# One order for all steps of a squared-ReLU MLP, and another tile order in its last block

## The chip, the cores and the metric

The kernel runs on one core of a Trainium2 chip. The metric is the time of one execution on the device in microseconds (us); a smaller one is better. The work of a core is done by TensorE (PE in the profile; its weight loads are the row PEld), VectorE (DVE), ScalarE (ACT), GpSimd (POOL) and SyncE (SP, which here only asks for transfers). Each of them runs its own instructions in order; they wait for one another by semaphores. Every matmul product lands in PSUM, which has eight banks of 512 float32 values a partition.

## What is computed

A trunk of two layers on 512 tokens of width 1024. Each layer has a mixer (latent attention in layer 0, gated linear attention in layer 1) and then this MLP:

```
def sq_relu_mlp(xn, w_up, w_down):          # 1024 -> 4096 -> 1024
    hid = jnp.square(jax.nn.relu(xn @ w_up))
    return hid @ w_down

x = x + sq_relu_mlp(rms_norm(x, norm_mlp[i]), mlp_w_up[i], mlp_w_down[i])
...
return rms_norm(x, final_norm)               # after layer 1
```

All of it is float32. The change touches the two MLPs and nothing else.

## The kernel before

**Numbers in two halves.** A float32 operand goes to TensorE as two pieces, a rounded high half and the rest as a low half. `split` makes them: ACT copies with rounding (L124), then VectorE subtracts (L127; L870 and L871 for a negated operand). A product of two such operands takes three matmuls (high x high, high x low, low x high). For weights the halves are the tiles `wh` and `wl`, four rooms of each (`piece`); for hidden values there are four rooms in `parts_room`, used in turn by `parts_of_quad`.

**Blocks and steps.** The 4096 hidden columns are cut into eight blocks of 512 (`FB`). `up_first` makes the first hidden block, `q11, q12, q21, q22` (two halves of its columns by two halves of the tokens). Then seven steps, b = 0 to 6, each do two things: the *down* products of the hidden block at hand, and the *up* products that make the next hidden block. Both use a scheme with 7 products in place of 8 (Strassen's, in Winograd's form), so a step has seven `up_product` and seven `down_product`, with sums of weights and of hidden values between them. The eighth block is done last, by itself.

**Up products.** They are called by the piece of tokens that they use: "11", "T1", "T2", "21", "T3", "22", "T4" (`quad`). Their weights are `A1` (with halves a11, a12), `A2` (s3, a22) and `S1` (s1); a11 becomes a11 + S1 before "T2", and a12 becomes a12 + a11 before "22". Their matmuls are at L993. Results are in banks of tag "u" (four of them), copied by ACT from one to another where two sums share a beginning (`y` is begun as a copy of `z`, `w2` as one of `w`), and end in `finish`: a rectifier on VectorE (L885) and a square on ACT (L886).

**Down products.** Weights `d11`, `d12`, `dS1`, `dS3`, `d22`; results go to the two-bank tiles "d" and "e" (or a pair of "u" banks), and from there to five running totals `S11, S12, S21, SU, S5`. Their matmuls are at L1006 in layer 0 (256 columns a matmul) and L1013 in layer 1 (512 columns).

**Two orders of a step.** `step`, used for b = 0 in each layer, alternates up and down products. `step_in_halves`, used for b = 1 to 6, does all up products first and then all down products. In both, `after(name)` follows the last use of a weight tile and asks for the next step's weights in the same place. `S1`, `A2`, `dS1` and `dS3` are each a sum of two parts of the weights: SP asks for the first, and POOL then asks for a transfer that adds the second.

**The start of an MLP.** `up_first` ends in four rectifiers (L900) and squares (L902). `quadrants` makes T1 to T4 on VectorE. `residual` loads the totals with the residual stream; in layer 1 by 32 transposes on TensorE (L941). Then the first step's weights are fetched in a list's order.

**The last block of layer 1.** The seventh step's last down products complete S12 (L1189) and then SU (L1192); S11 is complete before (L1179). `parts_of_quad` splits the four hidden quarters. For each of two column halves c and four tiles t of 128 tokens, `row(t, c)` adds 12 matmuls (L1303) to a bank that ACT has loaded with the total: for c = 0 S12 in "e" (tiles 2 and 3, L1272) and S11 in "d" (tiles 0 and 1, L1288), for c = 1 "u" banks (L1294). Then come the final norm's sums (L1306 to L1317) and the two stores of the tile (L1321, L1323).

The order in which each engine gets its instructions is set when the kernel is built: a planner takes them in the order of the program, and puts ahead those that are ready while others wait, by its own costs.

Of the kernel before, what the change touches and what calls it, by code (L numbers as in the profile page):

```python
# [14 lines left out]
AF = mybir.ActivationFunctionType  # L15
# [35 lines left out]
def trunk_kernel(ctx: ExitStack, tc: tile.TileContext, t_in: dict, out: bass.AP):  # L51
# [24 lines left out]
    def bank(tag):  # L76
        return psum["pool"].tile([P, 512], F32, tag=f"ps_{tag}", bufs=psum["banks"][tag], name=uname("ps"))

    def two_banks(tag):
        return psum["pool"].tile([P, 1024], F32, tag=f"ps_{tag}", bufs=1, name=uname("ps2"))  # L80
# [749 lines left out]
    def mlp(layer, nrm, nxt=None):  # L830
# [17 lines left out]
        def laid(t):  # L848
            return t.rearrange("p (j t) -> p j t", t=TH) if nxt else t
# [135 lines left out]
        def up_product(t, a, q, start):  # L985
            w = piece(a, KH, 256, at=AT_UP)
            for j in range(2):
                o = t[:, j * TH : (j + 1) * TH]
                for k in range(KH):
                    wh, wl = cut(w, slice(None), k, slice(j * P, (j + 1) * P))  # L990
                    xh, xl = quad[q][k][:, 0], quad[q][k][:, 1]
                    for n, (a_, x_) in enumerate(((wh, xh), (wh, xl), (wl, xh))):
                        PE.matmul(o, a_, x_, start=start and j == 0 and k == 0 and n == 0, stop=k == KH - 1 and n == 2, skip_group_check=True)  # L993
# [21 lines left out]

        def step(b, q, r, after):
            (q11, q12), (q21, q22) = q

            def begun(src):
                t = two_banks("e")  # L1020
                ACT.activation(t, src, AF.Copy)
                return t

            def add(total, t):
                DVE.tensor_tensor(total, laid(t), total, ALU.add)

            def onto(tag, total, a, parts, fresh=False):
                t = two_banks(tag)
                if not fresh:
                    ACT.activation(laid(t), total, AF.Copy)  # L1030
                down_product(t, a, parts, fresh)
                ACT.activation(total, laid(t), AF.Copy)

            A1, A2, s1 = W["A1"], W["A2"], W["S1"]
            a11, a12, s3, a22 = A1[:, :KH], A1[:, KH:], A2[:, :KH], A2[:, KH:]
            d11, d12, ds1, ds3, d22 = (W[n] for n in ("d11", "d12", "dS1", "dS3", "d22"))

            z = bank("u")
            up_product(z, a11, "11", True)
            y = bank("u")  # L1040
            ACT.activation(y, z, AF.Copy)

            d = two_banks("d")
            down_product(d, d11, parts_of_quad(q11), True)
            e = begun(d)

            up_product(y, a12, "21", False)
            finish(y, 0, 0, r)
            DVE.tensor_tensor(a11, s1, a11, ALU.add)

            down_product(e, d12, parts_of_quad(q21), False)
            add(S11, e)
            DVE.tensor_tensor(d11, ds1, d11, ALU.add)
            DVE.tensor_tensor(q12, q22, q12, ALU.subtract)
            DVE.tensor_tensor(q11, q11, q12, ALU.add)

            part = {"e": e}

            def down_11():
                down_product(d, d11, parts_of_quad(q11, -1.0), False)  # L1060
                part["e"] = begun(d)
                DVE.tensor_tensor(d12, d11, d12, ALU.add)
                after("d11")

            def up_t2():
                up_product(z, a11, "T2", False)
                u = part["u"] = tmp()
                ACT.activation(u, z, AF.Copy)
                DVE.tensor_tensor(a12, a11, a12, ALU.add)

            def up_t1():
                w = part["w"] = bank("u")
                up_product(w, s1, "T1", True)
                w2 = part["w2"] = bank("u")
                ACT.activation(w2, w, AF.Copy)  # L1075
                after("S1")

            def down_22():
                e = part["e"]
                down_product(e, d12, parts_of_quad(q22), False)  # L1080
                add(S12, e)
                after("d12")

            def down_12():
                down_product(d, ds3, parts_of_quad(q12), False)
                add(SU, d)
                after("dS3")
                DVE.tensor_tensor(q22, q22, q11, ALU.subtract)

            def up_22():  # L1090
                w = part["w"]
                up_product(w, a12, "22", False)
                c = tmp()
                DVE.tensor_tensor(c, w, part["u"], ALU.add)
                finish(c, 0, 1, r)
                after("A1")

            def up_t3():
                up_product(z, s3, "T3", False)
                v = tmp()  # L1100
                ACT.activation(v, z, AF.Copy)  # L1101
                c = tmp()
                DVE.tensor_tensor(c, part["w2"], v, ALU.add)
                finish(c, 1, 1, r)

            def down_5():
                onto("e", S5, ds1, parts_of_quad(q22, -1.0), True)
                after("dS1")
                DVE.tensor_tensor(q21, q21, q11, ALU.subtract)

            def down_21():
                onto("d", S21, d22, parts_of_quad(q21, -1.0))
                after("d22")

            def up_t4():
                up_product(z, a22, "T4", False)
                finish(z, 1, 0, r)
                after("A2")

            for product in (up_t2, down_11, up_t1, down_22, up_22, up_t3, down_12, up_t4, down_5, down_21):  # L1120
                product()

        def step_in_halves(b, q, r, after):
            (q11, q12), (q21, q22) = q
            A1, A2, s1 = W["A1"], W["A2"], W["S1"]
            a11, a12, s3, a22 = A1[:, :KH], A1[:, KH:], A2[:, :KH], A2[:, KH:]
            d11, d12, ds1, ds3, d22 = (W[n] for n in ("d11", "d12", "dS1", "dS3", "d22"))
# [2 lines left out]
                ACT.activation(dst, src, AF.Copy)  # L1130
                return dst

            def onto(total, a, parts):
                pair = [bank("u"), bank("u")]
                cols = [part_of(total, i) for i in range(2)]
                for p, c in zip(pair, cols):
                    copied(laid(p), c)
                down_product(pair, a, parts, False)
                for p, c in zip(pair, cols):
                    copied(c, laid(p))  # L1140

            w, w2, z, y = (bank("u") for _ in range(4))
            up_product(z, a11, "11", True)
            copied(y, z)
# [21 lines left out]
            after("A2")  # L1166

            d = two_banks("d")
            down_product(d, d11, parts_of_quad(q11), True)
            e = copied(two_banks("e"), d)  # L1170
            DVE.tensor_tensor(d11, ds1, d11, ALU.add)
            DVE.tensor_tensor(q12, q22, q12, ALU.subtract)
# [10 lines left out]
            after("d11")  # L1183
            p22 = parts_of_quad(q22)
            DVE.tensor_tensor(q22, q22, q11, ALU.subtract)
            onto(S5, ds1, parts_of_quad(q22, -1.0))
            after("dS1")
            down_product(e, d12, p22, False)
            DVE.tensor_tensor(S12, laid(e), S12, ALU.add)  # L1189
# [5 lines left out]
        up_first(Q[0])  # L1195
        quadrants()
        residual()
        for name in ("S1", "dS1", "d11", "A1", "d12", "dS3", "A2", "d22"):
            fetch(0, name)
        last_raw, last, gain = [], [[], []], []  # L1200

# [31 lines left out]
        for b in range(NB - 1):  # L1233
            final = b == NB - 2

            def after(name, b=b, final=final):
                if final:
                    return before_next(name) if nxt else at_the_end(name)
                fetch(b + 1, name)

            (step_in_halves if b else step)(b, Q[b % 2], Q[(b + 1) % 2], after)

        q = Q[(NB - 1) % 2]
        if nxt:
# [23 lines left out]
            es.close()  # L1268
            return
        hid = {}  # L1270
        loaded = {1: two_banks("e")}
        ACT.activation(loaded[1], S12, AF.Copy)  # L1272
        for h, th in ((0, 0), (0, 1), (1, 1), (1, 0)):
            hid[h, th] = parts_of_quad(q[h][th])
        DVE.tensor_tensor(S21, S21, SU, ALU.add)
        DVE.tensor_tensor(SU, SU, S5, ALU.add)
        rounded(1)
        gain = gain[0]
        DVE.tensor_scalar(gain, gain, -0.5, None, ALU.mult)
        stats = [sm(3) for _ in range(NT)]  # L1280
        rows = {}
        for c in range(2):
            for th in (1, 0):
                total = (S11, S12, S21, SU)[2 * c + th]
                if c == 0:
                    if th not in loaded:
                        loaded[th] = two_banks("d")
                        ACT.activation(loaded[th], total, AF.Copy)  # L1288
                    o = loaded[th]
                for i in range(2):  # L1290
                    cs = slice(i * 512, (i + 1) * 512)
                    if c:
                        o = bank("u")
                        ACT.activation(o, total[:, cs], AF.Copy, scale=-1.0)  # L1294
                    rows[2 * th + i, c] = total[:, cs], o if c else o[:, cs]

        def row(t, c):
            y, o = rows[t, c]
# [24 lines left out]
            ACT.dma_start(out_t[:, :512], y_0)  # L1323

        for c in range(2):
            for t in (2, 3, 0, 1):
                row(t, c)
        es.close()

# [554 lines left out]
```

## Time and profile before

| | |
|---|---|
| time, median of 3 runs | 1043.18 us (1042.81 to 1043.26) |
| time of the profiled execution | 1042.52 us |
| its span, first to last instruction | 1040.8 us |
| mean granted TensorE clock | 0.999 |
| busy: TensorE, weight loads, VectorE, ScalarE, GpSimd | 99%, 89%, 84%, 67%, 11% |
| MLP of layer 0: first step, the step after it | 39.39 us, 38.08 us |
| MLP of layer 1: first step with its transposes, the step after it | 42.68 us, 38.16 us |
| last block, first to last matmul's end | 1012.01 to 1034.3 us |

All times in the profile count from the first instruction. A line number is that of the kernel before, and can be that of a helper which many places call. "Idle before <- releaser" is the time for which the engine had nothing to do ahead of the instruction, and what it was waiting for last. A matmul's end is modelled, and a matmul starts while the one before it is still draining, so the distance from start to start tells what one costs.

### The profile page before, as it was taken

How to read it: one execution, taken by the hardware profiler on the slowest of the kernel's cores; microseconds unless marked ns; L12 is line 12 of the kernel's file. 1: busy time of each engine (PE TensorE's matmuls, PEld its weight loads, DVE VectorE, ACT ScalarE, POOL GpSimd, SP SyncE). 2: the span in 40 equal slices, each digit the busy share in tenths (PEclk: the TensorE clock that was granted, in tenths of full speed). 3: DMA queues.
4: the chain of work that ended last, by engine and by line, in shares of the span. 5: the costliest groups of instructions: out<-in, count | busy, mean ns of one | idle time of the engine just before them, and what ended most of it. 6: DMA issues, size and time to landing. Idle time of an engine off the chain costs nothing.

```text
span 1040.8 us, 16839 instructions
## 1 busy us (share of the span) xinstructions
PE 1030.6 (99%) x6522; PEld 923.2 (89%) x6522; DVE 878.5 (84%) x1343; ACT 695.1 (67%) x1122; POOL 113.2 (11%) x128
## 2 busy tenths in 40 slices
PE   9999999999999999999999999999999999999997
PEld 8788888899999999998888888888889989989985
DVE  7889976899989989989686499469898899898993
ACT  7667754667776876785345565655677677677684
POOL 8400000401101111000000000000011101111000
PEclk9999999999999999999999999999999999999999
DMA  7401214759988778623313212164488777878422
GB/s 234 123 21 41 78 45 148 200 134 223 234 195 204 180 198 203 150 82 122 91 41 95 95 54 82 51 163 148 98 239 203 188 199 191 203 182 198 106 82 82
DMA packets 120001, 145.85 MB, mean 140 GB/s; under 512 B 9488, under 2 KB 86288, under 8 KB 119920
## 3 DMA queue, kind: packets, MB, share of 16 engines
q1 hardware_dynamic: 95424, 113.57, 34.2%
q0 software_dynamic: 22400, 29.36, 17.8%
q10 hardware_dynamic: 2096, 1.84, 0.6%
q8 instruction: 51, 0.84, 0.3%
q14 instruction: 30, 0.25, 0.1%
HBM read 142.39 MB, written 2.10 MB: 139 GB/s over the span
## 4 chain that ended last, share of the span: by engine, by line
PE 92%; DVE 4%; ACT 2%; DMA 1%; issue 1%; SPq 0%; ACTq 0%; DVEq 0%
PE ps L993 25%; PE ps L1006 12%; PE ps L1013 12%; PE ps L132 10%; PE ps L133 10%; PE ps L134 10%; PE ps L1303 2%; PE ps L1264 2%; PE ps L149 1%; PE ps L1523 1%; PE ps L436 1%; PE ps L1650 1%; DVE wl L127 1%; ACT wh L124 1%; DMA comb<-in_mlp_w_down_dram 1%
## 5 line engine op out<-in xcount | busy, mean ns | idle before, releaser
L124 ACT ACTIVATE wh<-wraw 128x1024 fp32r<-128x1024 f32 x139 | 146.3, 1056 | 108.6 <-issue 37.0
L127 DVE TENSOR_TENSOR wl<-wraw,wh 128x1024 fp32r<-128x1024 f32 x139 | 169.5, 1220 | 36.6 <-ACT wh L124 35.8
L993 PE MATMUL ps<-T,wh 128*128 128x256 f32 x896 | 154.8, 275 | 0.1
L127 DVE TENSOR_TENSOR wl<-comb,wh 128x1024 fp32r<-128x1024 f32 x112 | 136.7, 1221 | 16.7 <-ACT wh L124 16.5
L124 ACT ACTIVATE wh<-comb 128x1024 fp32r<-128x1024 f32 x112 | 118.5, 1058 | 47.8 <-issue 28.8
L993 PEld LDWEIGHTS ps<-T,wh 128*128 128x128 f32 x896 | 135.1, 188 | 0.5 <-ACT tmp L1101 0.3
L993 PE MATMUL ps<-T,wl 128*128 128x256 f32 x448 | 123.3, 275 | 0.0
L1013 PE MATMUL ps<-wh,set 128*128 128x512 f32 x392 | 122.8, 390 | 0.2 <-ACT set L124 0.2
L993 PE MATMUL ps<-set,wh 128*128 128x256 f32 x672 | 117.0, 276 | 0.3 <-ACT ps L1075 0.2
L132 PE MATMUL ps<-set,wh 128*128 128x512 f32 x280 | 109.6, 391 | 0.0
L133 PE MATMUL ps<-set,wh 128*128 128x512 f32 x280 | 109.5, 391 | 0.0
L134 PE MATMUL ps<-set,wl 128*128 128x512 f32 x280 | 109.2, 390 | 0.0
L1006 PE MATMUL ps<-hidden_parts,wh 128*128 128x256 f32 x784 | 106.6, 275 | 0.0
L993 PEld LDWEIGHTS ps<-set,wh 128*128 128x128 f32 x672 | 101.9, 188 | 1.4 <-ACT ps L1075 0.4
L1006 PEld LDWEIGHTS ps<-hidden_parts,wh 128*128 128x128 f32 x784 | 97.0, 188 | 0.0
L993 PE MATMUL ps<-set,wl 128*128 128x256 f32 x336 | 92.6, 276 | 0.0
L1013 PEld LDWEIGHTS ps<-wh,set 128*128 128x128 f32 x392 | 73.5, 188 | 15.3 <-ACT set L124 0.4
L993 PEld LDWEIGHTS ps<-T,wl 128*128 128x128 f32 x448 | 84.1, 188 | 0.0
L1013 PE MATMUL ps<-wl,set 128*128 128x512 f32 x196 | 76.3, 389 | 0.0
L993 PEld LDWEIGHTS ps<-set,wl 128*128 128x128 f32 x336 | 63.1, 188 | 0.0
L134 PEld LDWEIGHTS ps<-set,wl 128*128 128x128 f32 x280 | 52.6, 188 | 11.0
L133 PEld LDWEIGHTS ps<-set,wh 128*128 128x128 f32 x280 | 52.6, 188 | 10.9 <-DVE set L765 0.2
(426 smaller groups left out, 2209.8 us busy)
## 6 DMA issues: line engine op xcount, KB each, us to landing
comb<-in_mlp_w_down_dram SPq DMA_DIRECT2D x74, 512.0 KB, 4.4
wraw<-in_mlp_w_up_dram SPq DMA_DIRECT2D x18, 1024.0 KB, 5.6
wraw<-in_mlp_w_up_dram SPq DMA_DIRECT2D x28, 512.0 KB, 5.8
comb<-in_mlp_w_down_dram POOLq DMA_DIRECT2D x28, 512.0 KB, 6.8
wraw<-in_gla_w_in_dram SPq DMA_DIRECT2D x12, 1024.0 KB, 5.2
comb<-in_mlp_w_up_dram SPq DMA_DIRECT2D x14, 512.0 KB, 4.6
comb<-in_mlp_w_up_dram POOLq DMA_DIRECT2D x14, 512.0 KB, 7.3
wraw<-in_mlp_w_up_dram POOLq DMA_DIRECT2D x14, 512.0 KB, 7.6
```

The lines of the kernel that those rows point to most:

```text
L124: order(ACT.activation(hi, src, AF.Copy))
L127: lo_eng.tensor_tensor(lo, src, f(hi), ALU.subtract)
L132: PE.matmul(psum, wh, xh, start=start, stop=False)
L133: PE.matmul(psum, wh, xl, start=False, stop=False)
L134: PE.matmul(psum, wl, xh, start=False, stop=stop)
L149: PE.transpose(psum, src, ident[: src.shape[0], : src.shape[0]])
L436: PE.matmul(p, w[:, i, j * P : (j + 1) * P], x, start=start, stop=stop)
L993: PE.matmul(o, a_, x_, start=start and j == 0 and k == 0 and n == 0, stop=k == KH - 1 and n == 2, skip_group_check=True)
L1006: PE.matmul(o, w_[:, k, j * P : (j + 1) * P], x_[:, ts], start=opens, stop=k == 1 and n == 2, skip_group_check=True)
L1013: PE.matmul(o, x_, w_, start=start and k == 0 and n == 0, stop=k == 1 and n == 2, skip_group_check=True)
L1264: PE.matmul(p, a, x, start=k == 0 and n == 0, stop=k == 3 and n == 2)
L1303: PE.matmul(o, a, b_, start=False, stop=k == 3 and n == 2, skip_group_check=True)
```

## The change

`step` is dropped, and `step_in_halves` takes its name and is used for every b. Three things are fitted to that:

- For b = 0 the split of `q11` stands ahead of the up products (`p11`); for b = 1 to 6 it stays at the first down product.
- `onto`, which loads a total into a pair of banks, adds a product and copies it back, can leave the loading out; for b = 0 it does so with S5, which is empty.
- The first step's weights are fetched in the order A1, S1, A2, d11, dS1, d22, d12, dS3.

In the last block of layer 1 the tiles go in the order 0, 1, 2, 3. The banks are loaded (`seed`) with S11 in two "u" banks for tiles 0 and 1, and S12 in the left half of "e" and the left half of "d" for tiles 2 and 3; for c = 1 in "u" banks as before, S21 first. The hidden quarters are split in the order (0, 0), (0, 1), (1, 0), (1, 1).

```diff
-        def step(b, q, r, after):
...
-            for product in (up_t2, down_11, up_t1, down_22, up_22, up_t3, down_12, up_t4, down_5, down_21):
-                product()
-
-        def step_in_halves(b, q, r, after):
+        def step(b, q, r, after):
...
-            def onto(total, a, parts):
+            def onto(total, a, parts, fresh=False):
                 pair = [bank("u"), bank("u")]
                 cols = [part_of(total, i) for i in range(2)]
-                for p, c in zip(pair, cols):
-                    copied(laid(p), c)
-                down_product(pair, a, parts, False)
+                if not fresh:
+                    for p, c in zip(pair, cols):
+                        copied(laid(p), c)
+                down_product(pair, a, parts, fresh)
...
+            p11 = None if b else parts_of_quad(q11)
             w, w2, z, y = (bank("u") for _ in range(4))
...
-            down_product(d, d11, parts_of_quad(q11), True)
+            down_product(d, d11, p11 or parts_of_quad(q11), True)
...
-            onto(S5, ds1, parts_of_quad(q22, -1.0))
+            onto(S5, ds1, parts_of_quad(q22, -1.0), b == 0)
...
-        for name in ("S1", "dS1", "d11", "A1", "d12", "dS3", "A2", "d22"):
+        for name in ("A1", "S1", "A2", "d11", "dS1", "d22", "d12", "dS3"):
             fetch(0, name)
...
-            (step_in_halves if b else step)(b, Q[b % 2], Q[(b + 1) % 2], after)
+            step(b, Q[b % 2], Q[(b + 1) % 2], after)
...
-        loaded = {1: two_banks("e")}
-        ACT.activation(loaded[1], S12, AF.Copy)
-        for h, th in ((0, 0), (0, 1), (1, 1), (1, 0)):
+        rows = {}
+
+        def seed(o, total, th, c, sign=1.0):
+            for i in range(2):
+                cs = slice(i * 512, (i + 1) * 512)
+                rows[2 * th + i, c] = total[:, cs], o[i]
+                ACT.activation(o[i], total[:, cs], AF.Copy, scale=sign)
+
+        seed([bank("u"), bank("u")], S11, 0, 0)
+        for h, th in ((0, 0), (0, 1), (1, 0), (1, 1)):
             hid[h, th] = parts_of_quad(q[h][th])
+        seed([split_banks("e")[0], split_banks("d")[0]], S12, 1, 0)
...
+        seed([bank("u"), bank("u")], S21, 0, 1, -1.0)
+        seed([bank("u"), bank("u")], SU, 1, 1, -1.0)
...
         for c in range(2):
-            for t in (2, 3, 0, 1):
+            for t in range(NT):
                 row(t, c)
```

More of the change, by code (lines that the diff above doesn't have):

```diff
@@ L1017, in step @@
             (q11, q12), (q21, q22) = q
[L1019 to L1043, printed above, removed]
-            down_product(d, d11, parts_of_quad(q11), True)
-            e = begun(d)
-            up_product(y, a12, "21", False)
@@ L1048, in step @@
[L1048 to L1118, printed above, removed]
-            for product in (up_t2, down_11, up_t1, down_22, up_22, up_t3, down_12, up_t4, down_5, down_21):
-                product()
@@ L1123, in step_in_halves @@
-        def step_in_halves(b, q, r, after):
-            (q11, q12), (q21, q22) = q
             A1, A2, s1 = W["A1"], W["A2"], W["S1"]
@@ L1168, in step_in_halves @@
             d = two_banks("d")
-            down_product(d, d11, parts_of_quad(q11), True)
+            down_product(d, d11, p11 or parts_of_quad(q11), True)
             e = copied(two_banks("e"), d)
@@ L1280, in mlp @@
         stats = [sm(3) for _ in range(NT)]
[L1281 to L1295, printed above, removed]
+        seed([bank("u"), bank("u")], S21, 0, 1, -1.0)
+        seed([bank("u"), bank("u")], SU, 1, 1, -1.0)
         def row(t, c):
```

## The prediction

> **What bounds the kernel now.** I read the page's busy row first, then the waits of TensorE, then the stages by windows, then the timeline at each place that the diff touches.
>
> ```profile
> PE 1030.6 (99%) x6522; PEld 923.2 (89%) x6522; DVE 878.5 (84%) x1343; ACT 695.1 (67%) x1122; POOL 113.2 (11%) x128
> ...
> L124 ACT ACTIVATE wh<-wraw 128x1024 fp32r<-128x1024 f32 x139 | 146.3, 1056 | 108.6 <-issue 37.0
> ```
>
> TensorE is busy for 99% of the span (the second row, the high half of a weight split on ACT, is for later). No matmul is added or dropped by the diff, so the only thing to win or lose is TensorE's idle time. Three of its waits (us in total, times, longest) lie inside the diff:
>
> ```profile
> PE ps L1303 <- ACT ps L1272: 1.0, 1, 1.0
> ...
> PE ps L993 <- ACT ps L1075: 0.2, 1, 0.2
> PE ps L1013 <- ACT set L124: 0.2, 1, 0.2
> ```
>
> The first is the last block, the second is the first step of layer 0, the third the first step of layer 1. "Busy" hides part of each loss (a matmul's modelled end overlaps the gap), so I size them by the length of whole stages:
>
> ```profile
> core 0: us, PE busy (x) PEld busy (x) DVE busy (x) ACT busy (x) POOL busy (x), PEclk, DMA share, GB/s
> 206.35:245.74 39.39, 38.99 (x337) 38.39 (x336) 38.80 (x44) 27.44 (x36) 5.34 (x5) 1.00 0.69 179
> 245.74:283.82 38.08, 38.08 (x338) 38.08 (x337) 35.27 (x40) 29.21 (x41) 5.00 (x4) 1.00 0.85 207
> ...
> 739.22:781.90 42.68, 42.50 (x286) 38.64 (x284) 35.77 (x41) 30.74 (x40) 4.97 (x4) 1.00 0.68 172
> 781.90:820.06 38.16, 38.16 (x254) 34.85 (x252) 33.97 (x37) 29.01 (x41) 3.80 (x3) 1.00 0.79 198
> ```
>
> Rows one and three are the first steps (b = 0, the interleaved `step`) of the two layers; rows two and four are the steps behind them (b = 1, `step_in_halves`), where TensorE is busy for all of the stage. The granted clock (PEclk) is 1.00 throughout. The diff gives b = 0 the order of b = 1.
>
> **Layer 0, first step.** It is the same 336 matmuls in 39.39 us instead of 38.08: 1.31 us lost. One of the three places in the timeline (start, us, engine, line; [idle before <- releaser]):
>
> ```profile
> 211.36 0.61 PE L1006 MATMUL ps<-hidden_parts,wh 128*128 128x256 f32 x4
> 212.04 0.50 PE L993 MATMUL ps<-set,wh 128*128 128x256 f32 x2
> ...
> 211.40 0.58 ACT L1041 ACTIVATE ps<-ps 128x512 f32<-128x512 f32 x1
> ```
>
> Four matmuls from 211.36 would be done streaming at 211.81 (a product of 24 takes 38.08/14 = 2.72 us, 0.113 us each); the next product starts at 212.04, behind the copy of `z` to `y` on ACT, which is used by the product but one after. In the new order three products lie between that copy and its use (T1, T2, then 21), so this wait goes. What must be ready instead: the low halves of S1 by the second product (206.35 + 2.72 = 209.07), of T2 by 211.79, of a12 by 214.51. The VectorE queue at that place:
>
> ```profile
> 204.27 1.21 DVE L127 TENSOR_TENSOR wl<-wraw,wh 128x1024 fp32r<-128x1024 f32 x1
> 206.13 0.69 DVE L127 TENSOR_TENSOR hidden_parts<-set,hidden_parts 128x512 fp32r<-128x512 f32 x1 [0.65 <-ACT hidden_parts L124]
> 206.74 1.22 DVE L127 TENSOR_TENSOR wl<-comb,wh 128x1024 fp32r<-128x1024 f32 x1
> 207.88 1.22 DVE L127 TENSOR_TENSOR wl<-wraw,wh 128x1024 fp32r<-128x1024 f32 x1
> 209.01 0.68 DVE L900 SCALAR_TENSOR_TENSOR tmp<-ps,rstd 128x512 f32<-128x512 f32 x1
> 209.62 1.21 DVE L1049 TENSOR_TENSOR wraw<-comb,wraw 128x1024 f32<-128x1024 f32 x1
> ```
>
> Start to start, a wide instruction costs 1.14 us and a narrow one 0.61. From 205.40 (behind a11's low half) the queue needs the sum a11 + S1 (1.14), q11's low half (0.61, the split moved ahead), L900 (0.61) and S1's low half (1.14): 208.9, against 209.07. That is just in time even in the worst order of the four, and the 0.65 us idle row shows VectorE had room there. T2's low half (1.14 more) comes at 210.0 to 211.2, against 211.79, with its ACT half (1.06) beside it. Over the whole up half VectorE needs 7 splits, 2 sums, 4 rectifiers and 2 adds, 9 x 1.14 + 6 x 0.61 = 13.9 of 19.04 us; the down half 12 x 1.14 + 11 x 0.61 = 20.4 of 19.04. The up half's surplus of 5.1 us, less 1.2 for L900 and q11's split, is the lead for the down half's shortage of 1.4. So I take 1.2 of the 1.31 us, keeping 0.1 for S1's narrow margin. Bounds: 1.31 gained; at worst two down splits (the rooms of `wh`, four, that a11 and S1 leave) and q11's split go ahead of an up split at a time without slack, 2 x 1.14 + 0.61 = 2.9 us lost, 1.6 worse than now.
>
> **Its transfers.** A1, S1 and A2 now stand first in SP's queue, and S1's and A2's accumulating parts first in POOL's. Two rows of POOL's timeline, two of the transfers (last number: us from issue to landing), one of ACT's timeline:
>
> ```profile
> 183.28 1.45 POOL L982 DMA_DIRECT2D comb<-in_mlp_w_up_dram  x1 [103.62 <-DMA comb<-in_mlp_w_up_dram]
> ...
> 191.82 1.80 POOL L971 DMA_DIRECT2D wraw<-in_mlp_w_up_dram  x1
> ...
> comb<-in_mlp_w_up_dram POOLq DMA_DIRECT2D x1, 512.0 KB, 6.2
> wraw<-in_mlp_w_up_dram POOLq DMA_DIRECT2D x1, 512.0 KB, 7.9
> ...
> 1006.59 0.59 ACT L1130 ACTIVATE sum<-ps 128x512 f32<-128x512 f32 x1
> ```
>
> S1 is whole at 183.28 + 6.2 = 189.5 and A2 at 199.7; A2 is wanted by the fifth product, at 217.2. The down operands move behind them, and are first wanted at 225. They cost nothing: A2 could come 17 us later. The totals' copies in halves are six instructions of 0.59 (the last row, such a copy in a later step) for three wide ones; even with nothing set against them ACT gets 3.5 us more, and it is busy for 27.44 of 39.39: nothing.
>
> **Layer 1, first step.** Of the 42.68 us the next step's 38.16 is work, and so are 32 transposes:
>
> ```profile
> 739.22 1.91 PE L941 MATMUL ps<-ident,xT 128*128 128x128 f32 x16
> 740.89 0.48 PE L993 MATMUL ps<-set,wh 128*128 128x256 f32 x2
> ...
> 753.60 0.28 PE L993 MATMUL ps<-T,wh 128*128 128x256 f32 x1
> 754.05 0.50 PE L1013 MATMUL ps<-wh,set 128*128 128x512 f32 x1 [0.18 <-ACT set L124]
> ...
> 768.18 0.39 PE L993 MATMUL ps<-T,wh 128*128 128x256 f32 x2
> ...
> 770.90 0.40 PE L1013 MATMUL ps<-wh,set 128*128 128x512 f32 x1
> ...
> 773.66 0.40 PE L993 MATMUL ps<-T,wh 128*128 128x256 f32 x2
> ```
>
> 16 transposes from 739.22 to 740.89 are 1.67 us, 32 are 3.34; 42.68 - 38.16 - 3.34 = 1.18 us lost. The wait for q11's split at 753.60 is 0.45 - 0.11 = 0.34, and the matmul behind it reads 0.50 where the row at 770.90 has 0.40: 0.10. A product behind one of its own kind takes 2.72 (768.18 to 770.90), behind one of the other kind 2.76 (770.90 to 773.66); the interleaved order changes kind 10 times, the new one twice: 8 x 0.04 = 0.32. I take these three, 0.76; the other 0.42 lies where transposes and products alternate, which the change leaves. Bounds: 1.18 gained, 2.1 lost (the same 2.9 of new stall, less 0.76).
>
> **Last block.** Rows of the timeline, and one of the chain (start, us, what):
>
> ```profile
> 1010.63 0.39 PE L1013 MATMUL ps<-wh,set 128*128 128x512 f32 x1
> 1012.01 22.31 PE L1303 MATMUL ps<-set,set 128*128 128x512 f32 x96 [0.99 <-ACT ps L1272]
> ...
> 801.14 19.07 PE ps L1013 x84
> ...
> 1000.64 1.22 DVE L1179 TENSOR_TENSOR xT<-ps,xT 128x1024 f32<-128x1024 f32 x1
> ...
> 1008.47 0.68 DVE L127 TENSOR_TENSOR set<-set,set 128x512 fp32r<-128x512 f32 x1
> ...
> 1009.67 1.22 DVE L1189 TENSOR_TENSOR xT<-ps,xT 128x1024 f32<-128x1024 f32 x1
> ...
> 1022.89 11.00 PEld L1303 LDWEIGHTS ps<-set,set 128*128 128x128 f32 x49 [0.32 <-DVE xT L1309]
> ```
>
> A matmul of this width takes 19.07/84 = 0.227 us, so TensorE stands from 1010.86 to 1012.01, 1.15 us: tiles 2 and 3 open on S12, whose last sum (L1189) and copy (L1272) come behind the last product but one. S11 is complete at 1001.86 (L1179) and the last "u" banks are free at 1007.2 (L1130's row above), so its two copies (0.59 each) end long before 1010.86; the third hidden split, now (1, 0), is the one that ends at 1009.2 (1008.47 + 0.68). The 96 matmuls take 22.31 instead of 95 x 0.227 + 0.39 = 21.96: 0.35, most of it around 1022.89, where a weight load waits for a read of the other half of its bank pair. I take 1.4 of 1.15 + 0.35. Bounds: 1.5 gained; nothing, if another late input takes over. New waits: S12's right half goes to d once L1192 has read it (about 1013.2); queued behind it on ACT is tile 0's Square, due at 1013.6. The fourth hidden split and S12 are wanted by tile 2 at 1016.3. Everything behind the last matmul stays, so this gain reaches the end whole.
>
> **The sum.** 1.2 + 0.76 + 1.4 = 3.36 us. The profiled execution took 1042.52 us (span 1040.8), so 1039.16; the median of the runs is 0.66 above it, 1043.18, which gives 1039.8.
>
> **The rivals.**
>
> 1. Layer 0 keeps its loss, since VectorE is the bound there: 38.80 of 39.39 us busy. Against it: four of its 44 instructions there belong to the next step, which has 40. Gain 0.76 + 1.4: 1041.0. Chance 0.12.
>
> 2. Taking the halves apart is the loss itself. Rows:
>
> ```profile
> 245.74:264.78 19.04, 19.04 (x170) 19.04 (x169) 16.93 (x20) 13.74 (x19) 1.30 (x1) 1.00 0.85 199
> 264.78:283.82 19.04, 19.04 (x170) 19.04 (x169) 18.34 (x22) 15.47 (x23) 3.70 (x3) 1.00 0.85 215
> ```
>
> VectorE is at 16.93 in an up half, at 18.34 in a down half; a first step that has no lead loses the 1.4 us of shortage in each layer: layer 0 stays within 0.1 of now, layer 1 gets 0.6 worse, the last block 1.4 better: 1042.5. The Trainium skill, Perfetto Trace Analysis, section Optimization Strategy, says that where the most contended engine changes over time, interleaving the regimes may help; this change does the opposite. By that rule this rival holds; the trace disagrees so far as b = 1 goes, whose down half has TensorE at 19.04 of 19.04. Chance 0.10.
>
> 3. The last block's wait only changes its name: the hidden split that ends at 1009.2 slips by 3 us (it is wanted at 1012.2, by the seventh matmul), or a seed does. Gain 1.2 + 0.76: 1041.2. Chance 0.09.
>
> 4. Slower: down splits placed ahead of up splits starve both first up halves, 2.9 us each: 5.8 - 3.36 = 2.4 over, 1045.6. It decides from 5.5 us of new stall in all. For it: VectorE has no idle row after 206.13 in layer 0. Against it: in layer 1 it has many, 35.77 of 42.68. Chance 0.05.
>
> **How the numbers follow.** The forecast (all three parts, 1038.8 to 1041.0) has 0.62, and 0.02 is left for what I don't see. A measurement of this kernel can tell 0.2%, 2.1 us, from no change: 1041.1 is the line. Faster is 0.62 and half of rival 1, 0.68; same the other half, rivals 2 and 3 and a rest, 0.26; slower 0.06. The range runs from all 1.31 + 1.18 + 1.5 gained with 0.4 us of scatter, 1038.8, to 1042.2, which takes in rivals 1 and 3.
>
> **What would show it.** The two first steps by windows: 38.1 to 38.3 us and 41.8 to 42.0 us; no wait on L993 or L1013 in them; the kind of product changing twice; the first matmul of the last block 0.23 us behind the last product, and 21.96 us for its 96. It is wrong if TensorE waits for a `wl` at the second or third product of layer 0, or for a hidden part or a seed at the last block.

## The result, and the profile after

| | before | after |
|---|---|---|
| time, median | 1043.28 us (20 runs, 1041.06 to 1045.27) | 1041.55 us (20 runs, 1040.58 to 1042.24) |
| profiled execution, its span | 1042.52, 1040.8 us | 1041.60, 1039.9 us |
| layer 0, first step | 39.39 us | 39.03 us |
| layer 1, first step with its transposes | 42.68 us | 43.71 us |
| layer 1 from its second step to the end | 258.9 us | 257.4 us |

The ratio is 0.9982, 95% interval 0.9975 to 0.9989: 1.9 us less, where 3.4 had been forecast. The time lies within the forecast's range, but 0.45 us above its line of 1041.1 us, on the side that it called "same" (chance 0.26). With 20 runs of each kernel the interval still leaves out "no change". Only one of the three terms came out as worked out. The two profiled executions differ by 0.9 us; where the rest of the gain of the medians is, the experiments below show in part.

From the page of after, the busy row:

```profile
PE 1028.7 (99%) x6522; PEld 922.0 (89%) x6522; DVE 878.8 (85%) x1343; ACT 695.8 (67%) x1130; POOL 113.6 (11%) x128
```

The matmuls are the same 6522. The stages of after by windows: the two first steps, and the down half of the last step of layer 1 (window and length, busy time and count of each engine, granted clock, DMA share, GB/s):

```profile
206.04:245.07 39.03, 38.47 (x338) 38.28 (x337) 38.27 (x43) 29.55 (x42) 4.99 (x4) 1.00 0.76 189
738.78:782.49 43.71, 42.30 (x286) 38.22 (x285) 36.06 (x41) 31.50 (x44) 3.44 (x4) 1.00 0.64 157
...
992.37:1011.45 19.08, 19.08 (x87) 15.77 (x86) 17.46 (x23) 17.07 (x28) 0.00 (x0) 1.00 0.34 110
```

The later steps run without a gap, as before. The second row is the one to stop at: layer 1's first step got 1.03 us longer. TensorE's waits in after (us in total, times, longest):

```profile
PE ps L1013 <- ACT ps L1023: 1.4, 1, 1.4
...
PE ps L993 <- ACT tmp L1023: 0.6, 1, 0.6
```

The waits named in the prediction (L1272, L1075, and the split of q11 for L1013) are all gone. Two new ones stand in their place, one in each first step, both for the copies of `copied` (L1023). The last block, in TensorE's timeline of after:

```profile
1011.22 0.39 PE L1013 MATMUL ps<-wh,set 128*128 128x512 f32 x1
1011.45 21.92 PE L1193 MATMUL ps<-set,set 128*128 128x512 f32 x96
```

It begins 0.23 us behind the last product, and its 96 matmuls take 21.92 us.

**The wait in layer 0.** Timeline of after, VectorE, then ACT, then TensorE:

```profile
217.46 0.68 DVE L871 SCALAR_TENSOR_TENSOR hidden_parts<-set,hidden_parts 128x512 fp32r<-128x512 f32 x1
218.07 1.22 DVE L127 TENSOR_TENSOR wl<-wraw,wh 128x1024 fp32r<-128x1024 f32 x1
219.20 0.68 DVE L871 SCALAR_TENSOR_TENSOR hidden_parts<-set,hidden_parts 128x512 fp32r<-128x512 f32 x1
219.81 0.68 DVE L885 SCALAR_TENSOR_TENSOR tmp<-ps,rstd 128x512 f32<-128x512 f32 x1
...
220.52 0.63 ACT L886 ACTIVATE set<-tmp 128x512 f32<-128x512 f32 x1 [1.35 <-DVE tmp L885]
221.06 0.58 ACT L1023 ACTIVATE ps<-xT 128x512 f32<-128x512 f32 x1
221.58 1.05 ACT L124 ACTIVATE wh<-comb 128x1024 fp32r<-128x1024 f32 x1
222.54 0.58 ACT L1023 ACTIVATE tmp<-ps 128x512 f32<-128x512 f32 x1
...
222.33 0.28 PE L993 MATMUL ps<-set,wl 128*128 128x256 f32 x1
223.16 0.50 PE L993 MATMUL ps<-T,wh 128*128 128x256 f32 x2 [0.56 <-ACT tmp L1023]
```

Read it backwards. The last up product, "T4", goes on in the bank of "T3" and must wait until ACT has copied that bank to `v` (222.54), 0.72 us beyond TensorE's own pace. ACT is late because its queue stood for 1.35 us at the square of product "21", and that waited for the rectifier of "21" on VectorE (219.81), 2.6 us after the product's last matmul had ended (217.2). Ahead of the rectifier VectorE was doing work for the *down* half: two of those instructions are shown (L871, halves of -q21 and -q11), six of 0.61 us in all stand between 210.5 and 219.8.

**The wait in layer 1.** The same three engines of after:

```profile
765.01 1.28 DVE L127 TENSOR_TENSOR set<-set,set 128x512 fp32r<-128x512 f32 x2
766.22 0.68 DVE L1070 TENSOR_TENSOR set<-set,set 128x512 f32<-128x512 f32 x1
...
763.75 1.21 ACT L124 ACTIVATE set<-set 128x512 fp32r<-128x512 f32 x2
764.86 1.01 ACT L1023 ACTIVATE ps<-ps 128x1024 f32<-128x1024 f32 x1
...
764.13 0.39 PE L1013 MATMUL ps<-wh,set 128*128 128x512 f32 x1
765.92 0.50 PE L1013 MATMUL ps<-wh,set 128*128 128x512 f32 x1 [1.41 <-ACT ps L1023]
```

The first down product ends at 764.36, and the second (d12, into "e") begins with a copy of the first's result; that copy can only start then, starts 0.5 us later (ACT is at two late splits) and lasts 1.01 us, and TensorE has nothing else. In later steps the product onto S21 stands between the two and covers the copy (in the next step the same copy runs from 804.84 to 805.85, and TensorE has no gap). Here its operand -q21 was not there: q21 is overwritten in place (L1070), so that sum must wait until the split of q21 has read it (765.01), and the split, though q21 was whole at 740.4, stands on ACT behind all squares of the up half (763.75). So -q21 is whole only at 769.2. Why the planner put this split last in layer 1 and not in layer 0 was not found out.

### The profile page after: what moved, and what is told of

It reads as the page before. It is cut to its first block, busy times and chain, and to the rows that moved or that the text cites. A ratio compares the mean times of both kernels' runs of the same rounds, so it can differ in the third digit from the quotient of the medians.

```text
span 1039.9 us, 16853 instructions
## 1 busy us (share of the span) xinstructions
PE 1028.7 (99%) x6522; PEld 922.0 (89%) x6522; DVE 878.8 (85%) x1343; ACT 695.8 (67%) x1130; POOL 113.6 (11%) x128
## 4 chain that ended last, share of the span: by engine, by line
PE 88%; DVE 5%; ACT 3%; DMA 2%; issue 1%; SPq 0%; ACTq 0%; DVEq 0%
PE ps L993 26%; PE ps L1013 13%; PE ps L1006 12%; PE ps L132 10%; PE ps L134 10%; PE ps L133 10%; PE ps L1413 1%; PE ps L149 1%; PE ps L1193 1%; DVE wl L127 1%; DMA wraw<-in_mla_w_in_dram 1%; PE ps L1540 1%; ACT wh L124 1%; DVE acc L266 1%; PE ps L1159 1%
## 5 line engine op out<-in xcount | busy, mean ns | idle before, releaser
L1013 PE MATMUL ps<-wh,set 128*128 128x512 f32 x392 | 122.3, 390 | 1.4 <-ACT ps L1023 1.4
L1013 PEld LDWEIGHTS ps<-wh,set 128*128 128x128 f32 x392 | 73.6, 188 | 17.2 <-ACT ps L1023 1.8
L1013 PE MATMUL ps<-wl,set 128*128 128x512 f32 x196 | 76.1, 389 | 0.0
L134 PEld LDWEIGHTS ps<-set,wl 128*128 128x128 f32 x280 | 52.6, 188 | 11.2 <-DVE wl L127 0.2
```

Source lines behind the costliest of these rows:

```text
L134: PE.matmul(psum, wl, xh, start=False, stop=stop)
L1013: PE.matmul(o, x_, w_, start=start and k == 0 and n == 0, stop=k == 1 and n == 2, skip_group_check=True)
```

## The experiments

**The two parts of the change, one at a time.** First the kernel before with the new last block:

> The kernel before, with only the last block's part of the change (its first two tiles first, their banks and copies). If the last block is what won, as the trace of after shows it (its 96 products stand directly behind the last product, where 1.15 us of wait and 0.35 us between the products were before), this alone is 1.4 to 1.5 us below before, and the two first steps stay at 39.4 and 42.7 us. Rival: what the last block wins depends on the new steps ahead of it; then it is under 1 us.

Measured: 1042.12 us against 1043.14 of before, ratio 0.9993 (0.9984 to 1.0001). The time alone does not settle it: a gain of 1.0 us by the medians and 0.7 by the ratio, with an interval from 1.7 down to nothing. The trace does: from the second step of layer 1 to the end it takes 257.4 us, as after does, so the block's gain does not need the new steps. Then the kernel after with the old last block:

> The kernel after, with the old last block: only the steps and their order of fetches are changed. By the two traces (first step of layer 0 0.36 us shorter, first step of layer 1 1.03 us longer) it is about 0.7 us slower than before, 0.3 to 1.0 with the scatter. By the prediction (1.2 and 0.76 us won) it would be 2.0 us faster. If it is within 0.2 us of before, the two profiled executions differ by something besides these two steps.

Measured: 1042.38 us against 1043.14, ratio 0.9992 (0.9983 to 1.0001); not slower. Its own first steps, by windows, are those of after:

```profile
208.05:246.90 38.85, 38.38 (x337) 38.18 (x336) 38.09 (x43) 29.53 (x42) 4.55 (x4) 1.00 0.77 190
740.66:784.32 43.66, 42.25 (x286) 38.19 (x284) 36.05 (x41) 31.50 (x44) 3.76 (x4) 1.00 0.64 157
```

That points at the other kernel: 39.39 us may not be the usual length of the old first step of layer 0. The run with the old steps and the new last block showed 40.03.

**The kernel before, profiled again.**

> The kernel before, unchanged, profiled once more. It asks how far its own stages move from one execution to the next: layer 0's first step took 39.39 us in the profile of before and 40.04 us in the kernel with only the new last block, which has the same step. If the old step moves by itself, this one shows another length, anything from 39.4 to 40.1 us, while the new step, which took 39.03, 38.86 and 39.04 us in three kernels, does not move. If it does not move, it is 39.4 us again, layer 1's first step 42.7 us, and the last block's wait 1.15 us.

> As the one before it: a third profile of the kernel before. Of interest are the length of the two first steps (39.4 to 40.0 and 42.7 us so far), the wait ahead of the last block (1.15 us in before, 0.39 us in the kernel with only the new steps, whose last block is the same), and the first 12 us, where one execution took 0.43 us from product to product for a while and another 0.23 us.

Layer 0's first step by windows, in the first of the two (the other took 40.11 us):

```profile
206.48:246.73 40.25, 38.98 (x337) 38.38 (x336) 39.03 (x45) 27.98 (x38) 5.54 (x5) 1.00 0.66 174
```

So the old step moves by 0.9 us from one execution to the next, and the profile on which the prediction rests holds the shortest of four. Layer 1's step does not move (42.71 and 42.70 us). What moves it is on ACT. The same row in the timeline of before, and in the first of the two others (in brackets, how long ACT was idle ahead of it, and what ended that):

```profile
201.73 1.07 ACT L124 ACTIVATE wh<-comb 128x1024 fp32r<-128x1024 f32 x1 [2.40 <-DMA comb<-in_mlp_w_down_dram]
```

```profile
202.70 1.07 ACT L124 ACTIVATE wh<-comb 128x1024 fp32r<-128x1024 f32 x1 [3.25 <-DMA comb<-in_mlp_w_down_dram]
```

This is the split of d11, the operand of the old step's second product. ACT, whose queue is in order, stands until the load has landed:

| execution with the old step | split of d11 starts | step ends | difference | step |
|---|---|---|---|---|
| before | 201.73 | 245.74 | 44.01 | 39.39 |
| new last block only | 202.06 | 246.07 | 44.01 | 40.03 |
| before, third | 202.45 | 246.42 | 43.97 | 40.11 |
| before, again | 202.70 | 246.73 | 44.03 | 40.25 |

The end of the step follows the landing to within 0.06 us. (The next expectation counts from 0.06 us ahead of the split's start, so its distances are that much longer.) To move the landing on purpose, d11 and d12 exchange their rooms in the old step, so that d11's load is issued second:

```diff
-        home = {"S1": 0, "dS1": 1, "d11": 4, "d12": 3, "dS3": 2, "d22": 5}
+        home = {"S1": 0, "dS1": 1, "d11": 3, "d12": 4, "dS3": 2, "d22": 5}
```

> The old steps (and the new last block), with the rooms of the weights d11 and d12 exchanged, so that d11 is loaded as the second of the four late transfers instead of the first, about 1.7 us later. Theory: the old first step of layer 0 is set by the landing of d11, the operand of its second product, since in four executions its end came 44.07, 44.09, 44.03 and 44.07 us behind the end of ScalarE's wait for d11, while the step took 39.39 to 40.25 us. Then the wait ends about 1.7 us later (203.7 to 204.4 us), the step takes 41 to 42 us and its end is again 44.0 to 44.2 us behind it. Rival: the landing is not what sets it; then the step stays at 39.4 to 40.3 us.

The step by windows, and ACT's row:

```profile
205.32:246.59 41.27, 39.24 (x338) 38.45 (x337) 38.98 (x44) 29.97 (x42) 6.19 (x5) 1.00 0.65 170
```

```profile
203.57 1.07 ACT L124 ACTIVATE wh<-comb 128x1024 fp32r<-128x1024 f32 x1 [5.34 <-DMA comb<-in_mlp_w_down_dram]
```

The split starts at 203.57, 1.75 us ahead of the step's start, where it was 3.78 to 4.62 ahead in the four: 2.0 to 2.9 us later. The step is 1.0 to 1.9 us longer than in the four, which is the same less 1.0; so the length came out as expected, the distance did not: from the split to the step's end it is 43.02, not 44.0. The missing 1.0 us fits a weight split of 1.04 us that stood close behind d11's on ACT (203.31 in before) and that the planner now put behind the squares and q11's split (206.90). So the landing sets the old step, through what stands behind it on ACT. The new step wants d11 only at its second half.

The old last block varies in the same way: TensorE's wait ahead of it was 1.15 us in before and 1.24, 0.41 and 0.39 us in three others; ACT's split of a last-block weight began 4.31 and 4.39 us behind the issue of its load in the first two, 3.56 and 3.54 in the others. That it follows the landing is read from these four alone; it was not tried.

**Layer 1: the hidden values ahead.** The kernel after, and for b = 0 of layer 1, ahead of the up products:

```diff
             p11 = None if b else parts_of_quad(q11)
+            if b == 0 and not nxt:
+                DVE.tensor_tensor(q12, q22, q12, ALU.subtract)
+                DVE.tensor_tensor(q11, q11, q12, ALU.add)
+                p21 = parts_of_quad(q21)
+                DVE.tensor_tensor(q21, q21, q11, ALU.subtract)
+                m21 = parts_of_quad(q21, -1.0)
```

> The kernel after, with four sums and splits of the hidden values moved ahead of the up products in layer 1's first step alone, so that the product onto S21 has its operand in time. Theory: the 1.57 us of wait behind the first down product is the copy of d to e, which nothing covers, as the product that covers it in later steps waits for its late operand. Then the wait goes, the first step of layer 1 falls from 43.7 to 42.0 us, and the whole is 1.5 to 1.7 us below after (3.4 to 3.6 below before). Rival: VectorE and ScalarE are simply full in a step whose halves are not interleaved; then the work moved ahead only moves the wait into the up products, the step stays at 43 to 44 us and the time within 0.4 us of after.

Measured: 1039.44 us against 1043.14, ratio 0.9970 (0.9958 to 0.9981). Windows, then VectorE's rows of the in-place sum and of -q21's low half, in this kernel:

```profile
738.75:780.74 41.99, 41.94 (x286) 38.38 (x284) 36.83 (x41) 31.05 (x44) 2.82 (x3) 1.00 0.67 162
```

```profile
743.89 0.69 DVE L1043 TENSOR_TENSOR set<-set,set 128x512 f32<-128x512 f32 x1
...
745.91 0.68 DVE L871 SCALAR_TENSOR_TENSOR set<-set,set 128x512 fp32r<-128x512 f32 x1
```

-q21 is whole at 746.6 instead of 769.2, no wait is left, and the step is 41.99 us, 1.72 less. VectorE does no less in it than in after (36.83 against 36.06 us), so its load was not the bound. Then only one of the moved pairs, the split of q21:

```diff
+            p21 = parts_of_quad(q21) if b == 0 and not nxt else None
...
-            p21 = parts_of_quad(q21)
+            p21 = p21 or parts_of_quad(q21)
```

> The kernel after, with one of the five moved instruction pairs only: the split of q21 ahead of the up products in layer 1's first step, the sums and the split of -q21 as they were. Theory: the product that must stand between the first down product and its copy needs the split of -q21, which comes last in the chain of sums, so one split alone does not help: the step stays above 43.0 us, with a wait of 1 us or more behind the first down product. Rival, that the late split of q21 itself (763.75 us) is the cause: the wait goes and the step falls to 42.0 to 42.3 us.

```profile
738.74:781.40 42.66, 42.47 (x286) 38.22 (x284) 36.72 (x41) 31.13 (x43) 2.99 (x3) 1.00 0.65 158
```

```profile
744.00 0.69 DVE L1071 TENSOR_TENSOR set<-set,set 128x512 f32<-128x512 f32 x1
...
765.07 0.68 DVE L871 SCALAR_TENSOR_TENSOR set<-set,set 128x512 fp32r<-128x512 f32 x1
```

I expected that it would not help; it brought 1.05 of the 1.72 us. The in-place sum followed by itself (744.00 instead of 766.22): once the split has read q21, the planner can put the overwriting sum where there is room. What stayed late is -q21's own split (765.07): TensorE, now at the product onto S21, stops shortly for its high half (until 764.47) and again for its low half (until 765.81), and this is the remaining 0.67. The step thus lies between the theory (above 43.0) and the rival (42.0 to 42.3): the larger part is the late read of a value that is overwritten in place, the smaller one the last split in the chain.

**Layer 0: the split ahead.** The kernel after without q11's split ahead, in both layers (`p11 = None`):

> The kernel after without the first down operand split ahead of the up products; everything else stays. Theory: the split ahead is not what delays layer 0's last up product (five other narrow instructions still stand ahead of the rectifier of product 21), so layer 0's first step stays within 0.4 us of 39.0 us, with the wait at the same product. In layer 1 the first down product loses its ready operand, so the step is as long or longer: 43.7 to 44.5 us. Rival, that the split is what crowds VectorE: both steps get shorter by about a split's two instructions, 0.7 us or more.

```profile
205.79:244.01 38.22, 38.22 (x337) 38.19 (x336) 38.05 (x44) 29.68 (x42) 4.99 (x4) 1.00 0.79 192
737.47:786.37 48.90, 44.24 (x286) 39.27 (x285) 37.95 (x42) 32.03 (x45) 3.22 (x4) 0.97 0.56 138
763.42:767.70 4.28, 3.67 (x10) 2.60 (x9) 3.44 (x6) 0.13 (x1) 0.00 (x0) 0.60 0.57 153
```

The theory missed in both layers. In layer 0 the step falls to 38.22 us: without that split at the head of VectorE's queue, the rectifier of "21" comes 12.97 us behind the step's start instead of 13.77, and that is enough. In layer 1 it costs 5.2 us, far more than the 0.8 expected at most; the third row, a part of this, is told of further down. The split ahead is thus worth 5.2 us in layer 1 and costs 0.8 in layer 0. The same in the other direction, with the sums and splits of q21 and -q21 ahead in layer 0 as well:

> The kernel with layer 1's sums and splits ahead, and the same edit in layer 0 as well. Theory: in layer 0 VectorE has no idle time while the up products run, so narrow instructions put ahead delay the rectifier of product 21 or a low half as before: layer 0's first step is 39.0 us or longer, up to 40 us, where it is 38.1 us with that work held back; layer 1 stays at 42.0 us. Rival: what matters in both layers is that the operands of the second down product are early; then layer 0's step falls to 38.2 us as well.

```profile
206.29:245.28 38.99, 38.66 (x337) 38.26 (x336) 38.23 (x43) 29.55 (x42) 4.76 (x4) 1.00 0.78 190
738.98:780.98 42.00, 41.94 (x285) 38.38 (x284) 36.83 (x41) 31.07 (x44) 3.01 (x3) 1.00 0.65 157
```

What gains 1.7 us in layer 1 gains nothing in layer 0: TensorE now waits for two earlier copies on ACT, ahead of 212.06 and 217.96.

**Both layers mended, in two ways.** Layer 1 with the hidden values ahead; layer 0 with that work held behind the rectifier of "21":

```diff
+                with tc.issue_after(made21.ins) if b == 0 else nullcontext():
                     DVE.tensor_tensor(q12, q22, q12, ALU.subtract)
```

> As the kernel with layer 1's sums ahead, and in layer 0's first step the opposite: the sums and the splits of q21 and -q21 (five of the six narrow instructions that stand ahead of the rectifier of product 21 on VectorE) are held until that rectifier has been issued. Theory: the 0.9 us of wait ahead of the last up product of layer 0 comes from that rectifier being late (219.81 us for a product that was done at 217.1), through the in-order queue of ScalarE to the copy of product T3. Then the wait goes, the first step of layer 0 falls from 39.0 to 38.1 or 38.3 us, and the whole is 0.7 to 0.9 us below the kernel with layer 1's sums ahead. Rival: VectorE, without idle time from 205.8 to 227 us, is the bound; then the held work makes the second down product wait, the step stays at 38.8 to 39.3 us and the time within 0.3 us.

Measured: 1038.81 us against 1043.14, ratio 0.9962 (0.9949 to 0.9974). Windows, and the rectifier and the copy `v`:

```profile
205.40:243.54 38.14, 38.14 (x337) 38.13 (x336) 36.89 (x42) 29.56 (x42) 6.04 (x5) 1.00 0.78 192
737.27:779.26 41.99, 41.94 (x286) 38.38 (x284) 36.64 (x41) 31.05 (x44) 3.08 (x3) 1.00 0.68 164
```

```profile
216.58 0.68 DVE L885 SCALAR_TENSOR_TENSOR tmp<-ps,rstd 128x512 f32<-128x512 f32 x1
...
220.17 0.58 ACT L1024 ACTIVATE tmp<-ps 128x512 f32<-128x512 f32 x1
```

The rectifier starts 11.2 us behind the step's start instead of 13.8, the copy 14.8 instead of 16.5, and TensorE is busy for 38.14 of 38.14 us. The work held back does not make the down half wait. The other way is simpler, `p11 = None if b or nxt`, so the split ahead for layer 1 only:

> The kernel after, each layer's first step with what suits it: layer 0 without the first down operand split ahead (its step was 38.22 us that way), layer 1 with that split and the four sums and splits of the hidden values ahead (41.99 us). If the two places are independent, the first steps are 38.2 and 42.0 us, the whole 0.8 us below the kernel with layer 1's sums ahead alone, equal to the kernel that treats both layers (1038.8 us) within 0.3 us, and 4.2 us below before. If layer 1's gain needs something of layer 0's order, its step is not 42.0 us.

Measured: 1039.26 us against 1043.60, ratio 0.9957 (0.9943 to 0.9970).

```profile
206.38:244.61 38.23, 38.23 (x338) 38.20 (x337) 38.06 (x44) 29.70 (x42) 6.14 (x5) 1.00 0.77 191
738.18:780.17 41.99, 41.94 (x285) 38.38 (x284) 36.64 (x41) 31.06 (x44) 3.63 (x3) 1.00 0.68 163
```

Both are 4.3 us below before by the medians, and 2.1 and 2.6 us below the kernel after by the ratios; their intervals stay just clear of its own.

## Why the prediction was right in its range, and where its steps failed

**Last block: right.** 1.4 was taken of 1.5. Between the profiled executions it is 1.5 (258.9 - 257.4), of which 1.15 is the wait. Against the other executions of the old block it is 0.8 to 1.7: the old wait has two lengths, which go with a transfer, and the profile of before held the long one. No input took over (rival 3).

**Layer 0: right in what goes, mis-sized in what comes.** The three old waits went. The step "I take 1.2 of the 1.31 us, keeping 0.1 for S1's narrow margin" failed: S1 was in time (its low half was there at 207.05, for a product at 208.8), and the loss was at the other end of the half. I summed VectorE's work in the up half, 13.9 of 19.04 us, and called the surplus a lead for the down half. The sum was right, but a surplus is used by pulling work forward, and in an in-order queue what is pulled forward stands ahead of the rectifier for which ACT's queue waits, and with it the copy that frees a bank. It came back as 0.95 us (39.03 - 38.08). Measured gain: 0.36 against the profile shown, 0.9 against the mean of the four executions (39.95), and with the work held back 1.25 and 1.8.

That also settles rival 1. VectorE, busy for 38.27 of 39.03 us, looks like the bound, but the step takes 38.23 us with VectorE busy for 38.06 of it, and 38.14 with 36.89: its order was at fault, not its load.

**The transfers: "they cost nothing" was right for the new order, and missed what they cost in the old one.** The quoted row of `z`'s copy at 211.40 was traced back to VectorE's queue and no further; the row 10 us earlier, where ACT waits 2.40 us for d11, was not looked at.

**Layer 1: wrong in sign.** The three parts of the 0.76 us did go, and 0.69 of it is gained once the new wait is gone (42.68 - 41.99). But the step's form was taken over from b = 1, where every hidden value is old; "the same 2.9 of new stall" was placed at the low halves of up weights. The stall came at the first down product, from a copy that in later steps has a product to cover it and at b = 0 has not, since that product's operand came 5 us late. 43.71 instead of 41.9, of which 1.57 is this wait and 0.11 the slow restart behind it; with it gone, 41.99.

Rival 4's place stayed clear: no product of the up halves waits for a low half of a weight.

**Rival 2** gave 0.6 us of loss in layer 1, for taking the halves apart. The sign was right, the mechanism not: with the halves apart and -q21 early, TensorE is busy for 41.94 of 41.99 us. The rule of the Trainium skill that was set beside it (Perfetto Trace Analysis, section Optimization Strategy) says that mixing regimes may help. Taking them apart did cost 1.0 us here, but through one late operand; with that early, the step without mixing is 0.7 us shorter than the mixed one (41.99 against 42.68 to 42.71).

**The sum.** By the traces, against the mean of the old executions: layer 0 gains 0.9, layer 1 loses 1.0, the last block gains 1.2 (0.8 to 1.7), and layer 0's own last block, which the change does not touch, loses 0.27 (22.37 against 22.09 us; it is 22.1 to 22.2 again in the three kernels whose first step of layer 0 is mended). That makes 0.8. The ratio makes 1.9, with an interval from 1.1 to 2.6. A part of what is missing is in executions that no profile holds: the three profiled ones of before average 1042.9 us, 0.4 below its median. By the medians the two parts alone gave 1.0 (last block) and 0.8 (steps), which add up to the 1.7 of both, while by the traces the steps alone lose 0.4; so as far as those wide intervals tell, the missing gain belongs to the steps. The start of layer 0's first step moves from one execution and one kernel to the next (206.31 to 206.48 us in three profiles of before, 205.32 and 206.04 in two other kernels with the old step, 205.40 to 206.38 in seven with the new one and 208.05 in an eighth), in code whose text no kernel here changed. Whether the missing 1.1 us (0.3 to 1.8 by the interval) is this scatter stays open, and so does the cause of the 0.27.

**What was luck.** One term came out, one had the wrong sign and one was mostly lost again. That the time still fell into the range is luck in good part: the range reached up to 1042.2 for rivals 1 and 3, and neither of them is what happened; and the old first step of layer 0 is usually longer than in the profile that the forecast was worked out from, which gave back about half a microsecond that nobody had counted.

## What to carry to other kernels

An order that runs without a gap in the steady state can fail in its first turn, where values that are otherwise a turn old are new: go through the first turn's operands one by one, and look for the product that covered a copy. In an in-order queue the place of an instruction can make a wait where the sum of the work leaves room; a late reader of a buffer that is overwritten in place holds up all that follows the overwriting. And a stage whose engine waits for a transfer is not measured by one profile: take its length from several executions before a difference of 1 us is read from it.

## What the runs showed of the hardware

In the kernel without the split ahead TensorE stood for 2.65 us in layer 1. Its timeline there:

```profile
760.15 0.28 PE L993 MATMUL ps<-T,wl 128*128 128x256 f32 x1
763.08 0.50 PE L1013 MATMUL ps<-wh,set 128*128 128x512 f32 x1 [2.65 <-ACT set L124]
...
764.42 1.22 PE L1013 MATMUL ps<-wh,set 128*128 128x512 f32 x2 [0.61 <-DVE set L127]
765.44 0.63 PE L1013 MATMUL ps<-wl,set 128*128 128x512 f32 x1
```

Two matmuls run behind the wait, then TensorE stands for another 0.61 us. From 765.0 to 767.6 the matmuls go at 0.43 us instead of 0.227, and the granted clock of that stretch is 0.60 (third row of that kernel's windows above): 1.00 until 764.1, 0.50 from 764.2 to 767.5. The seven matmuls from 764.42 take 3.15 us; with the restart seen behind the 1.57 us (0.34 for the first) and 0.227 for each of the others they would take 1.70. So 1.45 of the 5.2 us lost are this. After the 1.57 us in the kernel after there is none of it: the matmuls behind 765.92 are 0.23 us apart again after the first, and the clock is 1.00. The Trainium skill, TensorE: Matmul & The Clock Gate, Part 1, puts the fall to half the clock behind at least one idle window of about 3.4 us. Here the longest idle time was 2.65 us, and the clock fell 3.9 us behind the last matmul ahead of it, with two matmuls in between; whether 2.65 us alone would have done it, no run shows.

The pace of 0.43 us was also seen at the very start of an execution. TensorE's timeline of the kernel with the new steps and the old last block, and the same matmuls in after:

```profile
5.90 1.22 PE L436 MATMUL ps<-set,wh 128*128 128x512 f32 x2 [0.52 <-ACT set L276]
...
7.78 1.91 PE L436 MATMUL ps<-set,wh 128*128 128x512 f32 x4
9.48 1.05 PE L436 MATMUL ps<-set,wl 128*128 128x512 f32 x2
```

```profile
6.69 1.09 PE L436 MATMUL ps<-set,wh 128*128 128x512 f32 x4
7.62 0.63 PE L436 MATMUL ps<-set,wl 128*128 128x512 f32 x2
```

Four matmuls take 1.70 us in the one (7.78 to 9.48) and 0.93 in the other. The first is 2.3 us behind from there on, and still 2.0 us at the first step of layer 0 (208.05 against 206.04). The granted clock reads 1.00 here in both, so that the cause is the same as above is not shown. It is hardly the kernel's doing: this execution, 1044.22 us, is the slowest of its kernel's 11 (median 1042.38), and two profiles of the kernel before differ in the same way (its first four matmuls at L436 take 1.78 us in the first, 5.45 to 7.23, and 1.09 in the second, 5.27 to 6.36). It is a second reason not to compare spans of two profiles where 1 us matters.
